# A two-layer streaming encoder: attention scores, transposes and values as a pipeline over query tiles

## The chip, the core and the metric

The kernel runs on one core of a Trainium2 chip. The metric is the device time of one execution in microseconds, the median over runs. The core's engines have queues of their own and meet through semaphores: TensorE (PE in the profile: matrix products, its weight loads shown apart as PEld), VectorE (DVE), ScalarE (ACT), GpSimd (POOL) and SyncE (SP), which here issues the DMAs. TensorE writes its results to PSUM, from where VectorE and ScalarE read them.

## What is computed

528 tokens (16 meta tokens and 512 others) of width 1024 pass through two layers in fp32. Each layer normalises, projects to many columns, and runs three branches of width 512, pooling, differential attention and RWKV-7 time mixing, which are gated, merged, projected and added; then comes a convolutional feed-forward block. The branch that matters here, cut to its core (4 heads, two maps c per head with 64 dimensions each, values of 128):

```python
q = partial_rope(q); k = partial_rope(k)          # (tokens, 4, 2, 64)
def block(qi, ci):                                # 128 queries at a time
    s = einsum('bqhcd,bkhcd->bhcqk', qi, k) * 64 ** -0.5
    s = where(chunk[keys] <= ci[queries], s, -inf)    # chunks of 64 tokens
    p = softmax(s)
    a = p[:, :, 0] - lam * p[:, :, 1]
    return einsum('bhqk,bkhe->bqhe', a, v)
o = rms_norm(o, subln_w, 1e-5) * (1.0 - lambda_init)
```

## The kernel before

Activations lie transposed, features on partitions and the 528 tokens along the free dimension. A projection (gemm, lines 137 to 153) multiplies weights split into a high and a low part of a reduced fp32 form (F32R) with activations split likewise: three products for each of 8 row blocks and each half of 264 tokens, 48 in all (24 for the branch projections, which have 4 row blocks). weights (lines 126 to 135) loads 512 columns by a DMA on SyncE's queue; ScalarE makes the high part, VectorE the low part. A gemm writes into one of two PSUM lanes, g and f, of one buffer each, or into the tile s.

attention_phase (line 225) runs through ATTORDER, a list of steps written out by hand. q is a head's three projections, with rope on q and k (head, rope); h its attention (attend); n normalises the heads that wait; w and m are a pooling window and its linear; r is renorm, which rebuilds the activations from the input, normalised; u0 and u1 are the branch projections (projections) of pooling and attention. The steps give priorities. A scheduler at build time fixes the order of each engine's queue: an instruction of a later step is put ahead of one of an earlier step that is not ready, as far as buffers allow. So the products of head h + 1 fill the gaps of the attention of head h.

attend transposes v and calls softmax_tile for the 16 meta queries (j = -1) and four tiles of 128 queries. For each tile and each of the two maps the scores are one fp32 product (two records in the profile) of 64 rows, the maps on partitions 0 to 63 and 64 to 127 (line 269); the last tile has 528 keys and needs two PSUM banks a map, so two rounds (line 285). VectorE masks with a memset, takes the maximum and scales it, ScalarE takes the exponential and the sum, VectorE inverts the sums, ScalarE scales the second map by the sum and -lambda (line 296), VectorE combines (line 297). Then TensorE transposes the result, the 16 meta keys apart (lines 300 and 307), ScalarE copies it to SBUF (302, 310), and TensorE multiplies by v: the meta keys as a product of 16 rows (311), the others as products of 128 (313). ScalarE squares for the norm, VectorE copies (316, 317). The scores' PSUM tile s has one buffer (pss), the tile c two (pc).

## Time and profile before

| | |
|---|---|
| median of 3 runs | 2026.38 us |
| lowest, highest | 2024.83, 2027.46 us |
| profiled execution | 2025.1 us, span 2023.3 us |
| TensorE busy | 1972.2 us, 97% of the span |
| VectorE busy | 1260.9 us, 62% |
| ScalarE busy | 903.6 us, 45% |
| GpSimd busy | 25.1 us, 1% |
| mean granted TensorE clock | 0.996 |

The profile is of one execution, so sums are made against its 2025.1 us. A group's busy time is the union of its instructions' times; a record of TensorE is longer than the distance to the next one's start, because products are pipelined. What a product costs is therefore read from the distance of starts in the timeline.

### The profile page before, as it was taken

The numbers are of one execution on the slowest core, as the hardware profiler recorded it, in microseconds if no ns is written. First come the engines' busy times: TensorE is split into PE (matmuls) and PEld (weight loads), VectorE is DVE, ScalarE is ACT, GpSimd is POOL, SyncE is SP. The second block draws the span as 40 slices with busy tenths as digits, with TensorE's granted clock in tenths as the row PEclk, the third lists the DMA queues.
The fourth block names the chain that finished last, engine by engine and source line by source line (L and its number), as shares of the span: only waits on it lengthen the run. The fifth ranks groups of instructions, "written<-read, shape, count | busy, mean of one in ns | idle before, by whom it ended". The sixth has DMA issues, their size and how long they took to land. (4 is left out here: it accounts for less than half of the span.)

```text
span 2023.3 us, 40763 instructions
## 1 busy us (share of the span) xinstructions
PE 1972.2 (97%) x16528; PEld 1843.4 (91%) x16528; DVE 1260.9 (62%) x2304; ACT 903.6 (45%) x1741; POOL 25.1 (1%) x138
## 2 busy tenths in 40 slices
PE   8999999999999999999999999999899999999998
PEld 7888987988899999999988889889889999999886
DVE  7676377864666777753366753779455667777532
ACT  5556355334434444432254564552343454444332
POOL 0000000000000000000000000010000000000000
PEclk9999999999999999999999999999899999999999
DMA  6114422452464222234342244234514652222332
GB/s 200 49 47 138 160 76 64 151 150 85 131 189 137 90 90 94 90 100 124 119 130 64 60 135 143 73 92 128 171 54 128 216 189 91 93 90 94 94 94 94
DMA packets 145068, 228.37 MB, mean 113 GB/s; under 512 B 35536, under 2 KB 45296, under 8 KB 144752
## 3 DMA queue, kind: packets, MB, share of 16 engines
q1 hardware_dynamic: 144880, 225.77, 35.6%
q8 instruction: 130, 2.13, 0.4%
q14 instruction: 58, 0.48, 0.1%
HBM read 190.94 MB, written 34.77 MB: 112 GB/s over the span
## 5 line engine op out<-in xcount | busy, mean ns | idle before, releaser
L133 ACT CAST whi<-raw 128x512 fp32r<-128x512 f32 x564 | 346.1, 616 | 687.8 <-PE f L150 260.3
L134 DVE TENSOR_TENSOR wlo<-raw,whi 128x512 fp32r<-128x512 f32 x564 | 384.6, 684 | 334.6 <-ACT whi L133 315.9
L150 PE MATMUL g<-xh,whi 128*128 128x264 f32 (+1 forms) x1632 | 343.1, 289 | 7.9 <-ACT whi L133 6.1
L150 PE MATMUL g<-xh,wlo 128*128 128x264 f32 (+1 forms) x1632 | 342.3, 288 | 0.0
L150 PE MATMUL g<-xl,whi 128*128 128x264 f32 (+1 forms) x1632 | 341.3, 288 | 0.7 <-DVE xl L179 0.7
L150 PE MATMUL f<-xh,wlo 128*128 128x264 f32 (+1 forms) x1472 | 311.0, 290 | 6.6 <-DVE wlo L134 6.6
L150 PE MATMUL f<-xl,whi 128*128 128x264 f32 (+1 forms) x1472 | 309.5, 288 | 1.2 <-issue 1.2
L150 PE MATMUL f<-xh,whi 128*128 128x264 f32 (+1 forms) x1472 | 306.8, 288 | 1.3 <-DVE pu L374 0.8
L150 PEld LDWEIGHTS g<-xh,whi 128*128 128x128 f32 x1632 | 256.1, 190 | 14.5 <-ACT whi L133 6.1
L150 PEld LDWEIGHTS g<-xh,wlo 128*128 128x128 f32 x1632 | 256.5, 190 | 5.9 <-issue 3.8
L150 PEld LDWEIGHTS g<-xl,whi 128*128 128x128 f32 x1632 | 255.5, 189 | 4.9 <-DVE xl L179 1.2
L150 PEld LDWEIGHTS f<-xh,wlo 128*128 128x128 f32 x1472 | 231.5, 190 | 14.8 <-DVE wlo L134 7.9
L150 PEld LDWEIGHTS f<-xl,whi 128*128 128x128 f32 x1472 | 231.3, 190 | 4.0 <-issue 1.5
L150 PEld LDWEIGHTS f<-xh,whi 128*128 128x128 f32 x1472 | 230.5, 190 | 3.8 <-DVE pu L374 1.0
L1001 DVE TENSOR_TENSOR u<-g,rstd 128x528 f32<-128x528 f32 (+1 forms) x44 | 30.9, 702 | 77.2 <-PE g L150 77.2
L1001 DVE TENSOR_TENSOR u<-f,rstd 128x528 f32<-128x528 f32 (+1 forms) x44 | 30.9, 702 | 31.2 <-PE f L150 31.2
L706 DVE TENSOR_TENSOR i<-i,i 128x1 f32<-128x1 f32 (+30 forms) x62 | 48.2, 778 | 1.5
L150 PE MATMUL g<-gb,whi 128*128 128x264 f32 (+1 forms) x256 | 42.4, 285 | 0.0
L150 PE MATMUL f<-gb,whi 128*128 128x264 f32 (+1 forms) x256 | 42.2, 285 | 0.0
L1016 ACT CAST ah<-cg 128x528 fp32r<-128x528 f32 (+1 forms) x44 | 27.7, 629 | 22.2 <-DVE cg L1014 22.2
L150 PE MATMUL g<-al,whi 128*128 128x264 f32 x176 | 35.9, 285 | 0.0
L150 PE MATMUL f<-al,whi 128*128 128x264 f32 x176 | 35.8, 285 | 0.0
(397 smaller groups left out, 3246.2 us busy)
## 6 DMA issues: line engine op xcount, KB each, us to landing
raw<-in_w_in_dram SPq DMA_DIRECT2D x216, 256.0 KB, 2.9
raw<-in_ffn_up_dram SPq DMA_DIRECT2D x176, 256.0 KB, 2.8
raw<-in_ffn_down_dram SPq DMA_DIRECT2D x84, 256.0 KB, 2.6
raw<-in_w_branch_dram SPq DMA_DIRECT2D x48, 256.0 KB, 2.7
raw<-in_w_out_dram SPq DMA_DIRECT2D x32, 256.0 KB, 2.9
md<-th SPq DMA_DIRECT2D x16, 264.0 KB, 2.1
mu<-md SPq DMA_DIRECT2D x8, 528.0 KB, 5.0
bon<-h SPq DMA_DIRECT2D x16, 264.0 KB, 2.0
```

Of the source, the lines that this page charges most:

```text
L133: nc.scalar.copy(hi, raw)
L134: nc.vector.tensor_tensor(lo, raw, hi.bitcast(F32), ALU.subtract)
L150: nc.tensor.matmul(ps[:, h, :nh], w[:, ks], x[k0 + k][:, c0 + h * nh:c0 + (h + 1) * nh], start=(k0 + k == 0 and j == 0), stop=(k0 + k == n ...
L706: nc.vector.tensor_tensor(tv, m[:lanes, 0:i, i].unsqueeze(1).broadcast_to([lanes, i, i]), xt[:lanes, 0:i, 0:i], ALU.mult)
L1001: nc.vector.tensor_tensor(B.v2(u[:, 2 + c0:]), ps, B.v2(rstd[:, c0:]), ALU.mult)
L1016: nc.scalar.copy(h, g)
```

## The change

softmax_tile goes. Its work is done by step, five of them per head, each with one chain of products that keep their order on TensorE (the manual dependencies named "one burst"): the scores of a tile, the values of the tile of three steps ago, in step 1 the transposes of v, and the transposes of the tile of two steps ago. step 0 does the first full tile and the meta queries together (with 128 query and 128 key columns for the latter, masked), steps 1 and 2 a tile each, steps 3 and 4 one map each of the last tile. normalise first runs steps without scores until the lag is empty.

Scores are now products over 128 rows in the reduced fp32 form. stacked puts the high part of a map's q on its own 64 partitions and the low part on the other 64. twice makes the high and the low part of k, and copies both to the other 64 partitions by a DMA on GpSimd's queue. Two products add up: with k's high part, and with its low part. The meta keys' values (vm) are padded with zeros to 128 rows. The maps are combined without the first scale (mix), which comes in when the values are read from PSUM, as a scale of the square and of the copy to o.

ATTORDER moves q3 and h3 ahead of normalise and of the pooling windows; there is one normalise for all four heads. The lanes of heads 1 to 3 alternate. Working tiles of rope, renorm and projections share one tag t with 6 buffers; the second weight pool has 2 raw buffers in place of 3.

The diff, without the removed body of softmax_tile and some removed lines of attend:

```diff
--- before.py
+++ after.py
@@ -245,109 +245,190 @@

         def rope(tidx, lane="g"):
             ps = B.gemm(B.ins["w_in"][l, tidx], xh, xl, 0, L, lane)
-            raw = T("qraw", 2)
+            raw = T("t", 6)
             nc.scalar.copy(B.v2(raw), ps)
-            q = T("q" if tidx < T_K else "k", 2)
+            q = T("t", 6)
             nc.vector.tensor_tensor(B.v2(q), ps, B.v2(ropec), ALU.mult)
-            sh = T("qsh", 2)
+            sh = T("t", 6)
             nc.vector.stream_shuffle(sh, raw, perm)
             nc.vector.tensor_tensor(sh, sh, ropes, ALU.mult)
             nc.vector.tensor_tensor(q, q, sh, ALU.add)
-            return q
...
+            return stacked(q) if tidx < T_K else twice(q)
+
+        LO, HI = slice(0, 64), slice(64, 128)
+
+        def stacked(q):
+
+            t = T("qs", 2, (128, 2, L), F32R)
+            for c, (own, other) in enumerate(((LO, HI), (HI, LO))):
+                nc.scalar.copy(t[own, c], q[own])
+                nc.vector.tensor_tensor(t[other, c], q[own], t[own, c].bitcast(F32), ALU.subtract)
+            return t
+
+        def twice(k):
+
+            t = T("ks", 2, (128, 2, 2, L), F32R)
+            for c, (own, other) in enumerate(((LO, HI), (HI, LO))):
+                nc.scalar.copy(t[own, c, 0], k[own])
+                nc.vector.tensor_tensor(t[own, c, 1], k[own], t[own, c, 0].bitcast(F32), ALU.subtract)
+                nc.gpsimd.dma_start(t[other, c], t[own, c])
+            return t
+
+        def scores(out, q, k, c, q0, keys):
+            return [nc.tensor.matmul(out, q[:, c, q0:q0 + 128], k[:, c, i, keys], start=(i == 0), stop=(i == 1))
+                    for i in range(2)]
+
+        qkv, waiting = {}, []
+        lag = [[], [], []]
+
+        def soft(S, c0, w, mask):
+
+            ps, e, sm, mx = S
+            for m in mask:
+                nc.vector.memset(m, NEG)
+            v = ps[:, :, c0:c0 + w]
+            nc.vector.tensor_reduce(mx, v, AX.X, ALU.max)
+            nc.vector.tensor_scalar(mx, mx, -0.125, None, ALU.mult)
+            for c in range(2):
+                nc.scalar.activation(e[c][:, :w], v[:, c], AF.Exp, bias=mx[:, c:c + 1], scale=0.125,
+                                     accum_out=sm[:, c:c + 1])
+
+        def mix(e, sm, w):
+
+            rs = T("rs", 8, (128, 2))
+            nc.vector.reciprocal(rs, sm)
+            nc.vector.scalar_tensor_tensor(rs[:, 1:2], rs[:, 1:2], nlam, sm[:, 0:1], ALU.mult, ALU.mult)
+            nc.vector.scalar_tensor_tensor(e[0][:, :w], e[1][:, :w], rs[:, 1:2], e[0][:, :w], ALU.mult, ALU.add)
+            return e[0], rs
+
+        def small():
+            return T("sm", 6, (128, 2)), T("mx", 4, (128, 2))
+
+        def step(H, i):
+
+
+            done = lag[2]
+            lag[2], lag[1], lag[0] = lag[1], lag[0], []
+            burst = []
+            ps = B.pss()
+            spare = [ps[:, b, 384:512] for b in range(2)]
+            new = []
+            if H:
+                q, k = H["qk"]
+                if i == 0:
+                    for c in range(2):
+                        burst += scores(ps[:, c, 0:144], q, k, c, META, slice(0, 144))
+                        burst += scores(ps[:, c, 144:272], q, k, c, 0, slice(0, 128))
+                elif i < 3:
+                    nk = META + 128 * (i + 1)
+                    for c in range(2):
+                        burst += scores(ps[:, c, :nk], q, k, c, META + 128 * i, slice(0, nk))
+                else:
                     for hf in range(2):
...
+                        burst += scores(ps[:, hf, :264], q, k, i - 3, META + 384, slice(hf * 264, hf * 264 + 264))
+            for t in done:
+                if "po" not in t["shared"]:
+                    t["shared"]["po"] = B.pc()
+                po = t["shared"]["po"][:, t["slot"]:t["slot"] + 128]
+                at, HH = t["at"], t["H"]
+                burst.append(nc.tensor.matmul(po, at[:, t["m"]:t["m"] + 128], HH["vm"], start=True, stop=not t["nb"]))
+                for b in range(t["nb"]):
+                    burst.append(nc.tensor.matmul(po, at[:, b * 128:b * 128 + 128], HH["vt"][:, b, :],
+                                                  start=False, stop=(b == t["nb"] - 1)))
+            if H and i == 1:
+                pv = B.pc()
+                v = H["v"]
+                for b in range(4):
+                    burst.append(nc.tensor.transpose(pv[:, b * 128:(b + 1) * 128],
+                                                     v[:, META + b * 128:META + (b + 1) * 128], B.ident))
+                burst.append(nc.tensor.transpose(spare[0], v[:, :128], B.ident))
+            if lag[2]:
+                pt = B.pc()
+                at = T("at", 2, (128, 640))
+                at_n = 0
+                for t in lag[2]:
+                    t["at"], t["m"] = at, t["off"] + t["nb"] * 128
+                    for b in range(t["nb"]):
+                        burst.append(nc.tensor.transpose(pt[:, b * 128:(b + 1) * 128],
+                                                         t["a"][:, META + b * 128:META + (b + 1) * 128], B.ident))
+                    dst = pt[:, t["m"]:t["m"] + 128] if t["m"] < 512 else spare[1]
+                    burst.append(nc.tensor.transpose(dst, t["a"][:, :128], B.ident))
+                    at_n = t["m"] + 128
+            for x, y in zip(burst, burst[1:]):
+                tc.add_manual_dep(y.ins, x.ins.name, mybir.DependencyInfo(
+                    mybir.DependencyClass.NoSync, mybir.DependencyReason.DATA), reason="one burst")
+
+            if H:
+                if i == 0:
+                    for c0, w, slot, mask in ((0, 144, 0, [ps[0:64, :, 80:144]]),
+                                              (144, 128, 128, [ps[:, :, 160:272]])):
+                        e = [T("e", 6), T("e", 6)]
+                        sm, mx = small()
+                        soft((ps, e, sm, mx), c0, w, mask)
+                        new.append((e, sm, w, slot))
+                elif i < 3:
+                    nk = META + 128 * (i + 1)
+                    e = [T("e", 6), T("e", 6)]
+                    sm, mx = small()
+                    soft((ps, e, sm, mx), 0, nk, [ps[0:64, :, nk - 64:nk]])
+                    new.append((e, sm, nk, 0))
+                else:
+                    c = i - 3
+                    if c == 0:
+                        H["wide"] = [T("e", 6), T("e", 6)], *small()
+                    e, sm, mx = H["wide"]
+                    nc.vector.memset(ps[0:64, 1, 200:264], NEG)
+                    nc.vector.tensor_reduce(mx[:, c:c + 1], ps[:, :, :264], AX.XY, ALU.max)
                     nc.vector.tensor_scalar(mx[:, c:c + 1], mx[:, c:c + 1], -0.125, None, ALU.mult)
...
+                    nc.scalar.activation(B.v2(e[c]), ps[:, :, :264], AF.Exp, bias=mx[:, c:c + 1],
                                          scale=0.125, accum_out=sm[:, c:c + 1])
...
+                    if c:
+                        new.append((e, sm, L, 0))
+            if H and i == 1:
+                H["vt"] = T("vt", 2, (128, 4, 128))
+                H["vm"] = T("vm", 2, (128, 128))
+                nc.gpsimd.memset(H["vm"], 0.0)
+                nc.scalar.copy(H["vt"], pv.rearrange("p (a b) -> p a b", a=4))
+                nc.scalar.copy(H["vm"][:META], spare[0][:META])
+            if lag[2]:
+                nc.scalar.copy(at[:, :min(at_n, 512)], pt[:, :min(at_n, 512)])
+                if at_n > 512:
+                    nc.scalar.copy(at[:, 512:], spare[1])
+            for t in done:
+                po = t["shared"]["po"][:, t["slot"]:t["slot"] + 128]
+                junk = T("junk", 1, (128, 128))
+                j, HH = t["j"], t["H"]
+                nc.scalar.activation(junk, po, AF.Square, scale=t["rs"][:, 0:1], accum_out=HH["ss"][:, j:j + 1])
+                nc.vector.tensor_scalar(HH["o"][:, j, :], po, t["rs"][:, 0:1], None, ALU.mult)
+            shared = {}
+            for e, sm, w, slot in new:
+                a, rs = mix(e, sm, w)
+                meta = slot == 128
+                lag[0].append(dict(a=a, rs=rs, H=H, shared=shared, slot=slot, nb=0 if meta else (w - META) // 128,
+                                   off=256 if meta else 0, j=0 if meta else (w - META) // 128))

         def head(h):
-            q = rope(T_Q + h)
-            k = rope(T_K + h, "g" if h else "f")
-            ps = B.gemm(B.ins["w_in"][l, T_V + h], xh, xl, 0, L, "g" if h else "s")
+            q = rope(T_Q + h, None if h else "g")
+            k = rope(T_K + h, None if h else "f")
+            ps = B.gemm(B.ins["w_in"][l, T_V + h], xh, xl, 0, L, None if h else "s")
             v = T("v", VB)
             nc.vector.tensor_tensor(B.v2(v), ps, B.v2(rstd), ALU.mult)
             qkv[h] = q, k, v

         def attend(h):
             q, k, v = qkv.pop(h)
...
             if not waiting:
                 waiting.append(T("ss", 2, (128, 4, 5)))
                 nc.gpsimd.memset(waiting[0], 1.0)
...
+            H = dict(qk=(q, k), v=v, o=T("o", OB, (128, 5, 128)), ss=waiting[0][:, len(waiting) - 1])
+            waiting.append((h, H["o"]))
+            for i in range(5):
+                step(H, i)

         def normalise():

+            while any(lag):
+                step(None, 0)
             rs = waiting.pop(0)
             nh = len(waiting)
             nc.scalar.activation(rs[:, :nh], rs[:, :nh], AF.Sqrt, bias=B.eps[1e-5], scale=1.0 / 128)
@@ -357,9 +438,10 @@
                 ss = rs[:, hi]
                 for j in range(5):
                     nq = 128 if j else META
-                    nc.vector.tensor_scalar(o[:nq, j, :], o[:nq, j, :], ss[:nq, j:j + 1], None, ALU.mult)
+                    nc.vector.tensor_scalar(o[:, j, :], o[:, j, :], ss[:, j:j + 1], None, ALU.mult)
                     c = (0, META, META + 128, 0, 128)[j]
-                    nc.tensor.transpose(pt[:, j // 3, c:c + nq], o[:nq, j, :], B.ident[:nq, :nq])
+
+                    nc.tensor.transpose(pt[:, j // 3, c:c + 128], o[:, j, :], B.ident)
                 w0 = META + 256
                 for i, (c, w) in enumerate(((0, w0), (w0, 256))):
                     B.split(bh[1][h][:, c:c + w], bl[1][h][:, c:c + w], pt[:, i, :w], sub)
@@ -395,7 +477,7 @@
         def renorm():

             for d in range(KT):
-                x = T("xr", 2)
+                x = T("t", 6)
                 nc.sync.dma_start(x, xsrc(d))
                 nc.vector.scalar_tensor_tensor(x, x, vec[:, V_NM + d:V_NM + d + 1], rstd, ALU.mult, ALU.mult)
                 h, lo = B.xtile("xh"), B.xtile("xl")
@@ -409,7 +491,7 @@
             for d in range(KT):
                 lane, pool = ("f", ap) if d % 2 else ("g", None)
                 up = B.gemm(B.ins["w_branch"][l, br, d], bh[br], bl[br], c0, n, lane, pool)
-                t = T("th", 3)[:, :n]
+                t = T("t", 6)[:, :n]
                 nc.scalar.copy(B.v2(t), up)
                 nc.sync.dma_start(merged_dram[d][:, br, :n], t)

@@ -969,12 +1051,12 @@
 ORDER = 'k0 k1 k2 k3 l0 n0 d0 i0 o0 p0 i1 d1 o1 p1 i2 d2 o2 p2 i3 d3 o3 p3 l1 g0 g1 g2 g3'
 MAINBUFS = (4, 3, 3)
 FILLBUFS = (3, 2, 2)
-WIDEBUFS = (3, 3, 3)
+WIDEBUFS = (2, 3, 3)
 CUT = 304
 WL = 3
 VB = 2
 OB = 4
-ATTORDER = 'q0 s0 h0 q1 h1 q2 h2 n0 w0 w1 m0 w2 m1 w3 m2 m3 q3 h3 n0 u0 r0 u1'
+ATTORDER = 'q0 s0 h0 q1 h1 q2 h2 q3 h3 n0 w0 w1 m0 w2 m1 w3 m2 m3 u0 r0 u1'

```

## Rows read from the trace of the kernel before

**Rows 1.** The page, part 1: busy time and share, instructions.
```profile
PE 1972.2 (97%) x16528; PEld 1843.4 (91%) x16528; DVE 1260.9 (62%) x2304; ACT 903.6 (45%) x1741; POOL 25.1 (1%) x138
```

**Rows 2.** Sums by stretch: stretch, its length, busy time per engine, clock, DMA.
```profile
24.40:220.90 196.50, 192.29 (x1400) 169.69 (x1399) 128.51 (x325) 105.35 (x280) 1.15 (x12) 1.00 0.29 94
1022.70:1223.40 200.70, 197.29 (x1451) 175.29 (x1450) 129.90 (x327) 107.26 (x282) 1.39 (x15) 1.00 0.31 98
300.00:350.00 50.00, 45.23 (x389) 39.25 (x387) 39.22 (x68) 27.72 (x51) 2.72 (x7) 1.00 0.23 66
350.00:400.00 50.00, 50.00 (x400) 48.97 (x400) 40.15 (x101) 17.87 (x32) 3.05 (x6) 1.00 0.47 149
1366.00:1416.00 50.00, 50.00 (x418) 50.00 (x417) 48.11 (x101) 14.57 (x25) 0.00 (x0) 1.00 0.41 127
```

**Rows 3.** Groups by form, TensorE, 24.4 to 220.9 us: count, busy, mean ns, idle.
```profile
L313 PE MATMUL c<-vt,at 128*128 128x128 f32 x80 | 11.9, 279 | 0.0
L285 PE MATMUL s<-k,q 64*128 64x264 f32 x32 | 9.2, 409 | 0.0
L311 PE MATMUL c<-vm,atm 16*128 16x128 f32 x32 | 7.7, 321 | 0.0
...
L269 PE MATMUL s<-k,q 64*128 64x400 f32 x16 | 3.8, 548 | 0.0
L269 PE MATMUL s<-k,q 64*128 64x272 f32 x16 | 2.9, 441 | 0.0
L269 PE MATMUL s<-k,q 64*128 64x144 f32 x16 | 2.1, 335 | 0.1
L311 PE MATMUL c<-vm,atm 16*16 16x128 f32 x8 | 1.5, 273 | 0.0
L269 PE MATMUL s<-k,q 64*16 64x16 f32 x16 | 0.9, 180 | 0.9 <-ACT vm L339 0.9
```

**Rows 4.** Timeline of TensorE: start, length of the group, line, form, records.
```profile
31.42 0.41 PE L150 MATMUL g<-xh,whi 128*128 128x264 f32 x2
...
35.57 0.22 PE L269 MATMUL s<-k,q 64*16 64x16 f32 x4 [0.93 <-ACT vm L339]
...
77.97 0.28 PE L150 MATMUL f<-xh,wlo 128*128 128x264 f32 x1
78.18 0.94 PE L269 MATMUL s<-k,q 64*128 64x400 f32 x4
79.05 0.39 PE L150 MATMUL f<-xh,wlo 128*128 128x264 f32 x1
79.28 0.28 PE L150 MATMUL f<-xh,whi 128*128 128x264 f32 x1
...
80.45 0.48 PE L311 MATMUL c<-vm,atm 16*128 16x128 f32 x2
80.86 0.39 PE L150 MATMUL g<-xh,whi 128*128 128x264 f32 x1
...
84.44 1.15 PE L285 MATMUL s<-k,q 64*128 64x264 f32 x4
```

**Rows 5.** Timeline of TensorE: the end of layer 0's stretch, and the last stage.
```profile
220.47 0.40 PE L150 MATMUL f<-bh,wlo 128*128 128x264 f32 x2
220.72 0.41 PE L150 MATMUL g<-xh,whi 128*128 128x264 f32 x2
...
1900.10 0.39 PE L1056 MATMUL g<-whi,ah 128*128 128x512 f32 x1
1900.33 0.40 PE L1056 MATMUL g<-whi,al 128*128 128x512 f32 x1
```

**Rows 6.** Groups by form, VectorE, 24.4 to 220.9 us.
```profile
L134 DVE TENSOR_TENSOR wlo<-raw,whi 128x512 fp32r<-128x512 f32 x45 | 30.9, 687 | 22.3 <-ACT whi L133 20.3 <-PE f L150 1.8
L403 DVE TENSOR_TENSOR xl<-xr,xh 128x528 fp32r<-128x528 f32 x8 | 5.6, 697 | 0.0
```

**Rows 7.** The page, part 6: DMA issues, count, KB each, us to landing.
```profile
md<-th SPq DMA_DIRECT2D x16, 264.0 KB, 2.1
```

More of the change, by code (lines that the diff above doesn't have):

```diff
@@ L311, in softmax_tile @@
-            nc.tensor.matmul(po[:nq, :128], atm[:, :nq], vm, start=True, stop=(nb == 0))
-            for b in range(nb):
-                nc.tensor.matmul(po[:, :128], at[:, b * 128:(b + 1) * 128], vt[:, b, :],
-                                 start=False, stop=(b == nb - 1))
-            junk = T("junk", 1, (128, 128))
-            nc.scalar.activation(junk[:nq], po[:nq, :128], AF.Square, accum_out=ss[:nq, j + 1:j + 2])
-            nc.vector.tensor_copy(o[:nq, j + 1, :], po[:nq, :128])
-        qkv, waiting = {}, []
+                    if c:
+                        new.append((e, sm, L, 0))
@@ L330, in attend @@
             q, k, v = qkv.pop(h)
-            pv = B.pss()
-            nc.tensor.transpose(pv[:META, 1, :128], v[:, :META], B.ident)
-            for b in range(4):
-                nc.tensor.transpose(pv[:, 0, b * 128:(b + 1) * 128],
-                                    v[:, META + b * 128:META + (b + 1) * 128], B.ident)
-            vt = T("vt", 2, (128, 4, 128))
-            vm = T("vm", 2, (META, 128))
-            nc.scalar.copy(vt, pv[:, 0, :].rearrange("p (a b) -> p a b", a=4))
-            nc.scalar.copy(vm, pv[:META, 1, :128])
-            o = T("o", OB, (128, 5, 128))
             if not waiting:
@@ L343, in attend @@
                 nc.gpsimd.memset(waiting[0], 1.0)
-            ss = waiting[0][:, len(waiting) - 1]
-            waiting.append((h, o))
-            for j in (-1, 0, 1, 2, 3):
-                softmax_tile(h, q, k, vt, vm, o, ss, j)
+            H = dict(qk=(q, k), v=v, o=T("o", OB, (128, 5, 128)), ss=waiting[0][:, len(waiting) - 1])
+            waiting.append((h, H["o"]))
+            for i in range(5):
+                step(H, i)
         def normalise():
+            while any(lag):
+                step(None, 0)
             rs = waiting.pop(0)
```

50 lines of the change are left out of this document (removed).

## The prediction

> **What bounds the kernel now.** I read the page's busy shares first: TensorE is busy for 97% of the span, no other engine for more than 62% [rows 1]. Then the sums by stretch, for the two attention stretches that the change touches: from the end of the norm's products to the last branch projection, 196.5 us in layer 0 and 200.7 us in layer 1, 397 us of 2023 [rows 2]. [...] TensorE is idle for only 196.50 - 192.29 = 4.2 us and 200.70 - 197.29 = 3.4 us of them, VectorE is busy for 65%. So the order of work by now hides the softmax behind products of the next head, and what is left to win is TensorE work itself, plus at most 7.6 us of idle time.
>
> A product of the projections costs 0.25 us for two of 264 columns, 0.122 us each [rows 5]. Sixteen gemms of 48 and sixteen of 24 make 1152 such products, 140 us of a stretch; the other 57 us are attention. The groups by form show what they are [rows 3]: the scores take 0.9 + 2.1 + 2.9 + 3.8 + 9.2 = 18.9 us a layer, the products of the 16 meta keys 7.7 + 1.5 = 9.2 us, the other values 11.9 us. The timeline adds what the groups don't show [rows 4]: the 64-row block of 77.97 to 79.28 starts 0.21 us after a single projection product (normal 0.12) and the single one after it keeps the next one waiting 0.23 us. So each 64-row block costs about 0.09 us going in and 0.10 us coming out, less some 0.07 us by which its last record outlasts the start of the next product.
>
> **The change part by part.** *Scores.* Per head the kernel before has six blocks. With 0.12 us of edges each, a layer's 24 cost 18.9 + 2.9 = 21.8 us. After, a tile's scores are two full-array products in the reduced fp32 form for each of two maps: high and low part of q stacked in 128 rows, against k's high and then its low part. No row shows such a product of scores, but the projections are of the same form: 0.122 us at 264 columns, and 0.23 us at 512 in the last stage [rows 5], so 0.00045 us a column between; this gives 0.125 us at 272 and 0.18 at 400. Below 264 columns nothing of this form is shown: between half of it, 0.06 us (columns alone), and 0.122 us (no gain from fewer columns); I take 0.10. A head then has 8 x 0.10 (first block and meta together) + 4 x 0.125 + 4 x 0.18 + 8 x 0.122 = 3.0 us, between 2.7 and 3.2. A layer: 12 us. Gain 9.8 us.
>
> *Meta keys.* The 16-row products come in 20 blocks a layer; the one at 80.45 lasts 0.41 us, with edges of about 0.2 us [rows 4]. 9.2 + 20 x 0.2 = 13.2 us. After, the meta rows are padded with zeros to 128 (vm), and each tile has one more ordinary fp32 product of two records. Eighty records of the other values took 11.9 us; with pipelining, their starts stand some 0.11 us apart, so 40 more cost 4.5 us. Gain 8.7 us.
>
> *Transposes, normalise.* Their number stays the same; the 16-row ones become full ones and no longer break the stream, and values and transposes now follow each other in one run. I put that at 1.5 us a layer (0 to 3). Together 20 us a layer, **40 us** in all, between 36 and 44.
>
> *What is added beside TensorE.* stacked and twice run four times each per layer, with two ScalarE copies and two VectorE subtractions of 528 columns each: 16 subtractions at 0.70 us, the row of the same form in renorm [rows 6], 11 us a layer. The meta tile is computed on 128 rows instead of 16 and has a larger mask: some 1.5 us more. ScalarE gets 16 copies and loses the 20 scalings of e and the 20 copies of atm; it comes out even. VectorE's load is what matters, so I work it out for the part of the stretch ahead of renorm and the projections. It has 128.5 us in all [rows 2]; renorm makes two rounds of eight operations, the one shown 5.6 us, so 11 us; the projections' weights are 16 of 45, 11 us [rows 6]. 106 are left, and 118.5 with what is added. TensorE needs there 196.5 - 16 x 24 x 0.122 = 149.7 us now, of it 4.2 idle; after 149.7 - 4.2 - 20 = 125.5. **VectorE goes from 71% to 94% of that part, if TensorE is never to wait.** This is where I expect part of the gain to go. How TensorE fares beside such a VectorE is seen in three stretches [rows 2]: VectorE at 78% and TensorE at 90% (300 to 350 us), 80% and 100% (350 to 400), 96% and 100% (1366 to 1416, where VectorE works on something TensorE needs only later). The new part resembles the first most, since each step goes from TensorE to VectorE to ScalarE and back, but it has more spare products to fill with. I take 93%: 125.5 / 0.93 = 135, 9.5 us of idle time a layer, 19 us in place of the 7.6 us now.
>
> *What is moved.* q3, k3 and v3 go ahead of the pool windows. Their weight loads go ahead of the windows' in SyncE's queue too, with the same number of loads; a transfer of this size takes about 2.1 us [rows 7], a gemm of two loads 5.8 us, so nothing waits for them. WIDEBUFS gives the windows one raw buffer less; two still hold a whole window's weights. What the move takes away is cover: every window and its pool linear use lane f, and behind the last window no head's products are left; window, sums and linear are a chain of some 4 to 5 us, which the last head's late steps and its transposes cover if they are still there. It is part of the 9.5 us. Head 0 starts later, by four copies and subtractions, about 4.5 us, and k's copy to the other half of the partitions. That is two transfers a head of 264 KB on GpSimd's queue. No row shows a transfer from there; on SyncE's queue that size takes the same 2.1 us, and I take twice that as the upper end. First scores at 35.6 us now [rows 4] would come at about 43; the products of head 1 last from 31.4 us to 49, so it stays covered, and from head 1 on the copies lie a whole head ahead. Behind them on GpSimd wait only small memsets (GpSimd is busy for 1.2 us of the stretch [rows 2]).
>
> **The sum** is made against the profiled execution, 2025.1 us (span 2023.3); the median of the runs is 1.3 us above it. 2025.1 - 40 - 7.6 + 19 = 1996.5. I say **1996 us**.
>
> **The rivals.** *A, the forecast*: TensorE stays the bound at a share of 88 to 99% of the part: 2025.1 - 40 - 7.6 + 2 x (1.3 to 17), 1980 to 2012; with the bounds of 36 and 44 us it reaches 1976. *B, VectorE takes over*: at a share of 85% for TensorE the idle time is 22 us a layer, 2021 us; centre 2013. The 94% speak for it; against it that VectorE's 96% was reached once beside a full TensorE [rows 2].
>
> *C, slower: the single scores buffer.* pss has one buffer, so scores of step i + 1 wait until both exponentials of step i have read theirs. From the scores at 78.18 to the next at 84.44 are 6.3 us [rows 4], the longest steps of a head. Head 0 starts at 43 us, and 20 steps, 2 to 3 to drain the lag, normalise (some 8 us) and the second half of the projections (23.4 us) follow: 43 + 23 P + 31.4. It equals the present end, 220.7 us, at P = 6.4 us a step. At 6.8 us the stretch is 10 us longer in each layer, 2045. For it: VectorE's queue is fuller, and the longest period now is near that. Against it: a step's own chain (scores 0.7, mask, maximum, two exponentials of 0.6 us and more) is 3 to 4 us, and the transposes and values no longer stand in it.
>
> *D, the products don't get cheaper*: the pairs of 64-row products now run partly side by side (four records of 400 columns in 0.87 us [rows 4]), and the change gives that up; if the new products cost like fp32 ones, twice as much, a head's scores would take 5.5 to 6 us, the 9.8 us a layer are gone, and 1996 becomes 2016. The rows of the projections speak against it. [...]
>
> [...]
>
> **How the numbers follow.** A 0.60, B 0.20, C 0.11, D 0.05, E 0.04. Below 1976 lies some 0.03 of A, above 2019 a fifth of B and all of C: the range 1976 to 2019 leaves out 0.18. A measurement of this kernel can tell 0.2%, 4 us, from no change. Of C some 0.03 and of B 0.02 fall within it: faster 0.87, same 0.05, slower 0.08.
>
> **What would show it.** Right: groups of scores in 128*128 form, eight products of 264 columns a head some 0.12 us apart; no 0.09 us ahead of them; stretches of 175 to 190 us; TensorE work lower by some 20 us each. For B, VectorE above 90% until renorm, and TensorE's waits put down to it. For C, starts of scores over 6 us apart, with ScalarE's exponentials as releaser. For D, starts 0.22 us apart. [...] Wrong altogether: time lost outside the two stretches, by a lower granted clock.

## The result and the profile after

| | before | after |
|---|---|---|
| median, in the same session | 2026.92 us | 2036.79 us (2033.87 to 2043.70) |
| profiled execution, its span | 2025.1, 2023.3 us | 2042.5, 2040.7 us |
| mean granted TensorE clock | 0.996 | 0.983 |

The ratio is 1.0058, with an interval of 1.0035 to 1.0081: slower by 0.6%. The forecast was 1996 us. The six executions spread by 10 us and go roughly with their granted clock, from 2033.9 us at 0.987 to 2043.7 at 0.982; the profiled one, 0.983, is the second longest, so it lost more to the clock than the median did.

The page, part 1, of the kernel after (busy time, share of the span, instructions):

```profile
PE 1962.8 (96%) x16528; PEld 1863.7 (91%) x16528; DVE 1286.2 (63%) x2342; ACT 898.9 (44%) x1695; POOL 34.2 (2%) x160
```

TensorE is busy for 9 us less than in [rows 1], yet the span is 17 us longer. So TensorE waits more, and the mean clock says that part of its busy time runs slower. The sums by stretch show where (stretch, length, busy time of PE, PEld, DVE, ACT and POOL with their counts, granted clock, DMA share, GB/s). The kernel after: both attention stretches, then layer 0's in three parts, then two short pieces of it.

```profile
24.40:229.80 205.40, 185.78 (x1400) 177.97 (x1399) 140.92 (x344) 103.75 (x257) 4.87 (x13) 0.95 0.33 100
1032.30:1239.80 207.50, 190.84 (x1446) 183.10 (x1445) 143.02 (x346) 104.43 (x259) 5.22 (x17) 0.95 0.35 105
24.40:138.00 113.60, 106.49 (x838) 103.25 (x837) 93.93 (x240) 68.07 (x190) 4.73 (x11) 0.98 0.30 88
138.00:183.00 45.00, 35.63 (x218) 31.28 (x217) 27.76 (x70) 16.19 (x35) 0.14 (x2) 0.85 0.15 45
183.00:229.80 46.80, 43.66 (x349) 43.44 (x348) 19.24 (x34) 19.49 (x34) 0.00 (x0) 0.96 0.54 181
145.50:148.90 3.40, 3.40 (x18) 3.40 (x18) 0.00 (x0) 0.75 (x2) 0.14 (x2) 0.50 0.00 0
172.80:183.10 10.30, 8.05 (x30) 6.52 (x30) 3.40 (x7) 1.82 (x3) 0.00 (x0) 0.50 0.16 48
```

The same three parts of the kernel before:

```profile
24.40:138.00 113.60, 110.78 (x787) 94.83 (x785) 78.29 (x204) 60.54 (x177) 0.22 (x2) 1.00 0.24 75
138.00:183.00 45.00, 43.79 (x321) 38.83 (x320) 38.03 (x89) 27.79 (x68) 0.10 (x1) 1.00 0.42 129
183.00:220.90 37.90, 37.72 (x297) 36.03 (x296) 12.19 (x34) 17.02 (x35) 0.83 (x9) 1.00 0.32 111
```

The stretches last 205.4 and 207.5 us, against 196.5 and 200.7 in [rows 2]; the rest of the kernel is the same within 2 us. The middle part, where now all pool windows stand, has 45.0 - 35.6 = 9.4 us of idle TensorE against 1.2, and a clock of 0.85 against 1.00. In the last two pieces the clock is 0.50: there a pair of projection products takes 0.44 us from start to start (179.29 to 179.73, below), at the full clock 0.24 (183.17 to 183.41). In the kernel before the clock is 1.00 throughout these stretches [rows 2].

For each stretch I count idle time, half of the busy time at the lower level (the loss), and the rest, which is work at the full clock. This is worked out from all records of TensorE in the stretches above, layer 0 / layer 1, in us. (Half is a little much: 0.44 against 0.24 us makes it 0.45, that is, 16 us of loss in all instead of 8.96 + 8.86 = 17.8.)

| kernel | length | idle | lost to the clock | work |
|---|---|---|---|---|
| before | 196.5 / 200.7 | 4.2 / 3.4 | 0 / 0 | 192.3 / 197.3 |
| after | 205.4 / 207.5 | 19.6 / 16.7 | 9.0 / 8.9 | 176.8 / 182.0 |

So the work fell by 15.4 us a layer, as the change is meant to do; 15.4 and 13.3 us of idle time and 9 us of lower clock came in. What TensorE waits for in the middle part (engine, line, releaser: us in total, times, longest), in the view of waits:

```profile
PE f L163 <- DVE pu L456: 2.4, 2, 1.8
PE f L150 <- DVE bl L179: 2.0, 2, 1.8
PE g L150 <- ACT bh L178: 1.6, 2, 0.8
PE s L444 <- DVE bl L179: 1.6, 2, 1.1
PE f L163 <- DVE pp L468: 1.5, 1, 1.5
```

L150 is gemm, L163 pool_linear, L456 and L468 are pool_window, L444 normalise. pu is a window's product as VectorE read it from PSUM, pp its finished sums; bh and bl are the high and low part that ScalarE and VectorE make of a linear or of normalise's transposes. So a window waits for lane f, which the last linear holds until VectorE has read it, and the linear waits for the window's sums. VectorE's load is no bound there: it is busy for 27.8 of 45 us. The last two linears in the timeline of TensorE (start, length of the group, in brackets the idle time ahead of it), at the end of which lie the two starts 0.44 us apart:

```profile
169.76 1.16 PE L163 MATMUL f<-pp,pool_w 128*128 128x264 f32 x4 [1.81 <-DVE pu L456]
171.71 0.51 PE L150 MATMUL g<-bh,whi 128*128 128x264 f32 x2 [0.79 <-ACT bh L178]
172.52 0.58 PE L150 MATMUL g<-bl,whi 128*128 128x264 f32 x2 [0.29 <-DVE bl L179]
...
174.99 2.10 PE L163 MATMUL f<-pp,pool_w 128*128 128x264 f32 x4 [1.46 <-DVE pp L468]
177.88 0.81 PE L150 MATMUL g<-bh,whi 128*128 128x264 f32 x2 [0.79 <-ACT bh L178]
...
179.29 0.64 PE L150 MATMUL g<-bh,wlo 128*128 128x264 f32 x2
179.73 0.64 PE L150 MATMUL f<-bh,whi 128*128 128x264 f32 x2
```

The groups by form, TensorE, 24.4 to 229.8 us, which answer [rows 3]:

```profile
L278 PE MATMUL s<-ks,qs 128*128 128x264 f32 x32 | 6.0, 308 | 0.4 <-ACT e L383 0.2
L278 PE MATMUL s<-ks,qs 128*128 128x400 f32 x16 | 3.9, 365 | 0.2 <-ACT at L396 0.2
L278 PE MATMUL s<-ks,qs 128*128 128x272 f32 x16 | 3.1, 315 | 2.8 <-DVE e L301 2.0 <-ACT e L293 0.8
```

And a burst in the timeline of TensorE (start, length of the group), which answers [rows 4]:

```profile
66.84 0.40 PE L150 MATMUL f<-xh,wlo 128*128 128x264 f32 x2
67.08 0.75 PE L278 MATMUL s<-ks,qs 128*128 128x264 f32 x4
67.66 0.38 PE L334 MATMUL c<-vm,at 128*128 128x128 f32 x2
...
68.66 0.27 PE L355 MATMUL c<-consts,e 128*128 128x128 f32 x1
68.69 0.49 PE L150 MATMUL f<-xh,whi 128*128 128x264 f32 x2
69.02 0.40 PE L150 MATMUL f<-xl,whi 128*128 128x264 f32 x2
```

The four scores take 0.58 us to the next start; the first pair of projection products behind the burst takes 0.33 instead of 0.24, but starts only 0.03 us behind the last transpose.

### The profile page after: what moved, and what is told of

It reads as the page before. It is cut to its first block, busy times and chain, and to the rows that moved or that the text cites. A ratio compares the mean times of both kernels' runs of the same rounds, so it can differ in the third digit from the quotient of the medians.

```text
span 2040.7 us, 40772 instructions
## 1 busy us (share of the span) xinstructions
PE 1962.8 (96%) x16528; PEld 1863.7 (91%) x16528; DVE 1286.2 (63%) x2342; ACT 898.9 (44%) x1695; POOL 34.2 (2%) x160
## 4 chain that ended last, share of the span: by engine, by line
PE 81%; DVE 11%; ACT 3%; issue 3%; DMA 2%; SPq 0%; POOL 0%; DVEq 0%; ACTq 0%; POOLq 0%
PE f L150 33%; PE g L150 30%; PE g L1138 3%; PE f L1138 3%; DVE wlo L134 2%; DVE i L788 1%; PE s L163 1%; PE s L278 1%; PE c L997 1%; DVE q L690 1%; DVE i L790 1%; PE s L977 1%; DMA ks<-ks 1%; ACT whi L133 1%; PE c L981 1%
## 5 line engine op out<-in xcount | busy, mean ns | idle before, releaser
L134 DVE TENSOR_TENSOR wlo<-raw,whi 128x512 fp32r<-128x512 f32 x564 | 384.1, 683 | 364.9 <-ACT whi L133 343.8
L150 PE MATMUL f<-xh,wlo 128*128 128x264 f32 (+1 forms) x1616 | 339.4, 290 | 7.9 <-DVE wlo L134 7.9
L150 PE MATMUL f<-xh,whi 128*128 128x264 f32 (+1 forms) x1616 | 340.6, 291 | 5.2 <-DVE bl L179 2.9
L150 PE MATMUL f<-xl,whi 128*128 128x264 f32 (+1 forms) x1616 | 340.5, 290 | 0.0
L150 PE MATMUL g<-xh,whi 128*128 128x264 f32 (+1 forms) x1488 | 308.6, 287 | 6.7 <-ACT whi L133 6.7
L150 PE MATMUL g<-xh,wlo 128*128 128x264 f32 (+1 forms) x1488 | 310.6, 288 | 0.0
L150 PE MATMUL g<-xl,whi 128*128 128x264 f32 (+1 forms) x1488 | 308.1, 287 | 0.6 <-DVE xl L179 0.6
L150 PEld LDWEIGHTS f<-xh,wlo 128*128 128x128 f32 x1616 | 256.3, 192 | 12.3 <-DVE wlo L134 9.2
L150 PEld LDWEIGHTS f<-xh,whi 128*128 128x128 f32 x1616 | 256.5, 192 | 8.4 <-DVE bl L179 3.5
L150 PEld LDWEIGHTS f<-xl,whi 128*128 128x128 f32 x1616 | 256.5, 192 | 2.3 <-issue 0.4
L150 PEld LDWEIGHTS g<-xh,whi 128*128 128x128 f32 x1488 | 233.0, 190 | 8.7 <-ACT whi L133 6.7
L150 PEld LDWEIGHTS g<-xh,wlo 128*128 128x128 f32 x1488 | 233.5, 190 | 2.9 <-issue 0.9
L150 PEld LDWEIGHTS g<-xl,whi 128*128 128x128 f32 x1488 | 232.5, 189 | 3.0 <-DVE xl L179 1.0
L1083 DVE TENSOR_TENSOR u<-g,rstd 128x528 f32<-128x528 f32 (+1 forms) x44 | 30.9, 702 | 53.4 <-PE g L150 53.4
L278 PE MATMUL s<-ks,qs 128*128 128x144 f32 (+3 forms) x192 | 35.3, 310 | 9.1 <-DMA ks<-ks 3.7
L150 PE MATMUL g<-gb,whi 128*128 128x264 f32 (+1 forms) x256 | 42.7, 286 | 0.0
L150 PE MATMUL f<-gb,whi 128*128 128x264 f32 (+1 forms) x256 | 42.2, 285 | 0.0
L278 PEld LDWEIGHTS s<-ks,qs 128*128 128x128 f32 x192 | 26.9, 192 | 14.5 <-ACT e L293 6.7
L150 PE MATMUL g<-bh,whi 128*128 128x264 f32 (+1 forms) x128 | 28.9, 310 | 10.8 <-ACT t L495 6.2
```

What stands on the lines that cost most here:

```text
L134: nc.vector.tensor_tensor(lo, raw, hi.bitcast(F32), ALU.subtract)
L150: nc.tensor.matmul(ps[:, h, :nh], w[:, ks], x[k0 + k][:, c0 + h * nh:c0 + (h + 1) * nh], start=(k0 + k == 0 and j == 0), stop=(k0 + k == n ...
L278: return [nc.tensor.matmul(out, q[:, c, q0:q0 + 128], k[:, c, i, keys], start=(i == 0), stop=(i == 1)) for i in range(2)]
L1083: nc.vector.tensor_tensor(B.v2(u[:, 2 + c0:]), ps, B.v2(rstd[:, c0:]), ALU.mult)
```

## The experiments

All ratios are to the kernel before, run in the same session; a1, b1 and so on are the runs. The theory after the result: the pipeline saves what it should, and the move of head 3 ahead of the windows, with the lanes that go with it, leaves TensorE without other products in the windows' part; the gaps then bring the lower clock. Rivals: VectorE's added work; the shared buffers t; GpSimd's copy of k.

**Order.** The changed kernel with the windows ahead of head 3, one normalise:

```diff
-ATTORDER = 'q0 s0 h0 q1 h1 q2 h2 q3 h3 n0 w0 w1 m0 w2 m1 w3 m2 m3 u0 r0 u1'
+ATTORDER = 'q0 s0 h0 q1 h1 q2 h2 w0 w1 m0 w2 m1 w3 m2 m3 q3 h3 n0 u0 r0 u1'
```

> The changed kernel with the pooling windows back ahead of head 3 (one normalise, after head 3). Theory 'cover': the changed kernel loses its time where the windows, all in lane f, run behind the last head with nothing beside them; in layer 0 TensorE idles 9 to 10 us between 125 and 180 us and the granted clock is at the lower level for 13.7 us there. Then this kernel is faster than the changed one by 2 x (9 idle + about 5 clock), some 28 us: 2005 to 2015 us against 2037, and faster than the kernel before by 10 us or more. Theory 'VectorE': the loss is VectorE's load of the pipeline, wherever the windows stand: 2030 us or more, with the idle time only moved.

Run a1: 2036.84 us, 1.0046 (1.0031 to 1.0061): as slow as the changed kernel. In its waits of layer 0 a linear now waits once for 4.5 us, ahead of k's copy:

```profile
PE f L163 <- DVE pp L468: 4.5, 1, 4.5
PE s L278 <- DMA ks<-ks: 4.1, 3, 2.3
```

Idle time is 21.1 and 15.4 us, as much as with the new order. So the order alone isn't what costs.

The kernel before with the changed kernel's order, and nothing else of the change:

```diff
-ATTORDER = 'q0 s0 h0 q1 h1 q2 h2 n0 w0 w1 m0 w2 m1 w3 m2 m3 q3 h3 n0 u0 r0 u1'
+ATTORDER = 'q0 s0 h0 q1 h1 q2 h2 q3 h3 n0 w0 w1 m0 w2 m1 w3 m2 m3 u0 r0 u1'
```

> The kernel before with the new order alone (windows behind head 3, one normalise), the old softmax tiles kept. Theory 'cover': the windows stand uncovered here too, slower than before by 8 to 25 us, with TensorE idle ahead of the pool linears and a lower clock there. Theory 'VectorE': VectorE has its old load, so within 5 us of before.

Run b1: 2062.53 us, 1.0173 (1.0156 to 1.0190). In the old pipeline the move alone costs 35 us: idle 14.8 and 13.0 us, 6.2 and 5.0 us lost to the clock, work nearly as before (192.5 and 198.4). The part of the windows:

```profile
24.90:138.00 113.10, 111.34 (x801) 95.94 (x800) 76.19 (x195) 59.15 (x176) 0.11 (x1) 1.00 0.24 76
138.00:190.00 52.00, 39.78 (x232) 31.17 (x232) 37.84 (x103) 25.34 (x68) 0.70 (x7) 0.89 0.16 47
```

Ahead of it all is as it was; in the 52 us TensorE idles for 12.2, and the clock is down. So the move makes such gaps without the pipeline too.

**Order and lanes.** Windows ahead of head 3, and q, k and v of heads 1 to 3 in lane g as before:

```diff
-            q = rope(T_Q + h, None if h else "g")
-            k = rope(T_K + h, None if h else "f")
-            ps = B.gemm(B.ins["w_in"][l, T_V + h], xh, xl, 0, L, None if h else "s")
+            q = rope(T_Q + h)
+            k = rope(T_K + h, "g" if h else "f")
+            ps = B.gemm(B.ins["w_in"][l, T_V + h], xh, xl, 0, L, "g" if h else "s")
```

> The changed kernel with the pooling windows back ahead of head 3 and with the projections of heads 1 to 3 in lane g again, as before; one normalise. With the order alone put back, the windows in lane f stood in the way of head 3's projections, which took that lane in turn. Theory 'cover', now as 'two lanes beside each other': windows in f beside head 3 in g keep TensorE fed; idle time of a stretch falls from 16 to 21 us to 8 to 12, the lower clock goes, 2005 to 2020 us. Theory 'VectorE': idle stays at 15 us or more, 2030 us or more.

Run a9: 2017.61 us, 0.9964 (0.9951 to 0.9976): 19 us less than the changed kernel. Layer 0's stretch and its middle part:

```profile
24.40:215.40 191.00, 178.91 (x1399) 172.91 (x1398) 141.40 (x344) 103.60 (x257) 4.97 (x13) 0.99 0.35 108
...
138.00:183.00 45.00, 43.48 (x345) 41.72 (x345) 28.68 (x83) 26.06 (x69) 1.13 (x3) 1.00 0.33 102
```

The middle part has 1.5 us of idle time in place of 9.4, and a full clock. Why the old order needs the old lanes is seen at the last two linears of layer 0, which stand at nearly the same time in both runs. In a1:

```profile
129.85 0.40 PE L150 MATMUL g<-xh,wlo 128*128 128x264 f32 x2
130.81 1.16 PE L163 MATMUL f<-pp,pool_w 128*128 128x264 f32 x4 [0.56 <-DVE pu L456]
136.43 2.10 PE L163 MATMUL f<-pp,pool_w 128*128 128x264 f32 x4 [4.46 <-DVE pp L468]
140.12 0.81 PE L150 MATMUL f<-xh,whi 128*128 128x264 f32 x2 [1.59 <-DVE bl L179]
```

In a9:

```profile
130.91 1.16 PE L163 MATMUL f<-pp,pool_w 128*128 128x264 f32 x4
131.70 0.60 PE L150 MATMUL g<-xl,whi 128*128 128x264 f32 x2
...
136.28 0.28 PE L150 MATMUL g<-xl,whi 128*128 128x264 f32 x1
136.62 1.13 PE L163 MATMUL f<-pp,pool_w 128*128 128x264 f32 x4
```

In both VectorE makes the last window's sums from 130.1 us to 136.3 (a1) and 136.5 (a9). In a9 the products of head 3 in lane g fill this time. In a1 lane g's products of head 3 are done at 130 us, its other two gemms have lane f, and the first of them starts only when the last linear has been read from f: 4.5 and 1.6 us idle. With the order of before as a whole (two normalises) it is the same (run a10):

```diff
+ATTORDER = 'q0 s0 h0 q1 h1 q2 h2 n0 w0 w1 m0 w2 m1 w3 m2 m3 q3 h3 n0 u0 r0 u1'
```

> The same with normalise called twice, exactly the order of the kernel before; the pipeline runs empty once more in the middle. Theory 'two lanes': like the run with one normalise, 2005 to 2020 us, and a little better if the late normalise is what head 3 waits for. Theory 'VectorE': 2030 us or more.

Run a10: 2018.57 us, 0.9962 (0.9950 to 0.9975). The fourth corner, the three lines of lanes above put back alone and the order left new:

> The changed kernel with only the lanes of heads 1 to 3 put back (q, k and v of these heads in lane g), its order left as it is, the windows behind head 3. It fills the fourth corner beside after (new order, new lanes, 2037), the kernel with the old order and new lanes (2037) and the one with both old (2018). Theory 'the two belong together': the old lanes need windows in lane f between the heads' gemms; with all windows at the end, the gemms of heads 1 to 3 follow each other in one lane and each waits until ScalarE and VectorE have read the one ahead of it: about 9 gemms a layer, 1 to 2 us each, so 2037 + 2 x (9 to 18) = 2055 to 2073, as the old kernel with the new order lost 35 us. Rival 'the alternating lanes are what costs': undoing them alone brings most of the 19 us, 2018 to 2025.

Run c1: 2045.46 us, 1.0098 (1.0069 to 1.0127). The four corners:

| | new lanes | old lanes |
|---|---|---|
| new order | 1.0058 | 1.0098 |
| old order | 1.0046 | 0.9964 |

Either edit alone brings nothing, both together bring 1%; with the old lanes the move costs the pipeline 28 us (c1 against a9). The verdict of c1 is the first theory's, but neither its size (2055 to 2073) nor its mechanism: the waits of 138 to 183 us are those of normalise and of the last window, not of gemms that follow each other in one lane. The last product of a head or a window is made at 160.5 us there; behind it only linears, normalise and projections are left.

```profile
PE s L444 <- DVE bl L179: 4.5, 2, 2.2
PE g L150 <- ACT bh L178: 2.4, 3, 0.8
PE s L444 <- DVE pp L467: 1.1, 1, 1.1
```

**Lanes of the windows.** Windows and linears of the changed kernel alternate between f and g:

```diff
-            ps = B.gemm(..., *(("g", None) if g > WL else ("f", ap)))
+            ps = B.gemm(..., *(("g", None) if g % 2 else ("f", ap)))
-            ps = B.fmm(B.psg("f"), poolw[:, g * 128:(g + 1) * 128], pooled, L)
+            ps = B.fmm(B.psg("gf"[(g + 1) % 2]), poolw[:, g * 128:(g + 1) * 128], pooled, L)
```

> The changed kernel, in its own order, with the windows taking lanes f and g in turn and each pool linear the lane of the other. Theory 'two lanes': most of the 9 us of idle time in the windows' tail goes and the lower clock after it, 2 x (6 to 12), 2012 to 2026 us. Theory 'VectorE': no gain over 5 us, since the sums of a window run on VectorE either way.

Run a4: 2035.85 us, 1.0051 (1.0038 to 1.0064): no gain. Idle is 17.6 and 20.5 us; in layer 0 normalise's transposes (4.5 us, for VectorE's bl) and the wait of a projection for its lane's copy behind renorm (3.3) lead. So the single lane of the windows is not the cause by itself.

**VectorE's load.** In the attention stretches the low part of the weights is not made:

```diff
         nc.scalar.copy(hi, raw)
+        if self.nolo:
+            return hi, hi
         nc.vector.tensor_tensor(lo, raw, hi.bitcast(F32), ALU.subtract)
```

> The changed kernel, in its own order, without VectorE's low part of the weights in the attention stretches: the products with it take the high part again, so TensorE has the same work, and VectorE loses 45 subtractions, 31 us of 141 us in each stretch. (The result then lacks the low part of these weights.) Theory 'VectorE': with its load at 110 us TensorE's idle time falls from 18 us to 8 us or less and the lower clock with it: 2005 to 2015 us. Theory 'cover': the windows' tail and the start of head 0 stay, idle 13 us or more, 2025 us or more.

Run a11: 2032.52 us, 1.0030 (1.0021 to 1.0040). VectorE falls from 141 and 143 to 118 us a stretch, below the 128.5 of before, and the idle time only from 19.6 and 16.7 to 14.3 and 12.3 us: 9.7 of the 28.7 us that the change added. VectorE's load is the smaller part of it.

**VectorE's work on GpSimd.** The 16 subtractions of stacked and twice:

```diff
-                nc.vector.tensor_tensor(t[other, c], q[own], t[own, c].bitcast(F32), ALU.subtract)
+                nc.gpsimd.tensor_tensor(t[other, c], q[own], t[own, c].bitcast(F32), ALU.subtract)
```

> The changed kernel with the 16 subtractions of stacked and twice per layer made by GpSimd instead of VectorE, which takes 11 us of 141 us off VectorE in each attention stretch. Theory 'VectorE': idle time falls by most of that, 2015 to 2025 us. Theory 'cover': the windows' tail stays as it is, within 6 us of the changed kernel, or slower if GpSimd's subtraction is so long that k comes late.

Run a6: 2054.53 us, 1.0134 (1.0117 to 1.0150): 18 us slower. A group of GpSimd, layer 0, in this run:

```profile
L273 POOL TENSOR_TENSOR ks<-t,ks 64x528 fp32r<-64x528 f32 x8 | 11.3, 1416 | 24.9 <-ACT ks L272 24.6
```

In the changed kernel VectorE made one of them in 0.70 us:

```profile
L273 DVE TENSOR_TENSOR ks<-t,ks 64x528 fp32r<-64x528 f32 x8 | 5.6, 700 | 0.2
```

On GpSimd one takes 1.42 us. It stands ahead of k's copy, and the scores of layer 0 wait for that copy for 5.4 us. And VectorE's busy time fell only from 140.9 to 138.8 us, though 11 us went away.

**The buffers.** The projections' copies get buffers of their own in the changed kernel:

```diff
-            raw = T("t", 6)
+            raw = T("t", 4)
...
-                t = T("t", 6)[:, :n]
+                t = T("th", 2)[:, :n]
```

> The changed kernel with the shared working tiles parted: four for rope and renorm, two of their own for the branch projections. In the changed kernel one projection product waits 3.1 us per layer for the copy of a lane, which stands behind renorm's use of the shared tiles, and a stretch of lower clock follows. If the sharing causes this wait, it goes: 2 x (3 + 1.5), 5 to 10 us faster than the changed kernel. If the wait has another cause (order of the queues alone), within 3 us of it.

Run a3: 2044.72 us, 1.0081 (1.0063 to 1.0098). The wait of 3.1 us behind renorm is gone, and idle time is 22.4 and 19.9 us: waits of 3.8 us in normalise and 3.7 and 3.3 us at the linears take its place. So the shared buffers are not the cause either.

**What comes on top of order and lanes.** The same split of buffers in the version with old order and lanes, once with one normalise and once with two, and then k's copy issued by SyncE:

```diff
-                nc.gpsimd.dma_start(t[other, c], t[own, c])
+                nc.sync.dma_start(t[other, c].bitcast(F32), t[own, c].bitcast(F32))
```

> The pipeline with the old order (one normalise) and old lanes, 2018, in which the buffers that rope, renorm and the projections share are split (four for rope and renorm, two for the projections' copies). In it TensorE waits 3.5 us for a projection's copy behind renorm in layer 0. If the sharing is the cause and nothing takes its place: 2018 less 3 us a layer and less 1 to 2 us of lower clock behind it, 2010 to 2014. If the copy waits because ScalarE and VectorE are full with renorm then, the wait stays or moves: 2016 to 2020, as it was in the changed kernel itself.

Run c2: 2020.69 us, 0.9968 (0.9956 to 0.9981), no gain.

> The same split of buffers with the order of the kernel before (two normalises), 2019 without the split. Same expectations: 2011 to 2015 if the sharing is the cause, 2016 to 2020 if the wait moves.

Run c3: 2013.44 us, 0.9932 (0.9910 to 0.9955), 5 us less than a10; the intervals of the two overlap.

> As the one with one normalise and split buffers, and the copy of k to the other half of the partitions issued by SyncE in place of GpSimd. If the 3.3 us that the copy takes to land from GpSimd's queue, or its wait to be issued, sets head 0's start: first scores 1 to 2 us earlier in each layer, 2 to 4 us less than the version without it. Rival: on SyncE's queue the copy stands in order among the loads of weights and waits for VectorE's halves of k there, so loads behind it come late: 0 to 10 us more.

Run c4: 2010.97 us, 0.9923 (0.9899 to 0.9947), the lowest median here. Its two stretches, of its fastest execution:

```profile
24.60:213.90 189.30, 179.19 (x1399) 171.80 (x1398) 140.17 (x344) 102.39 (x257) 1.56 (x14) 1.00 0.34 109
1016.70:1208.00 191.30, 183.95 (x1450) 177.45 (x1449) 141.40 (x346) 104.17 (x259) 1.58 (x14) 1.00 0.36 114
```

The first scores come at 43.99 us, against 45.66 without SyncE's copy: the size expected. The gain of 10 us is more than that. In the profiled executions, 12 us apart, some 3.5 us lie outside the stretches and 4 us in them are lower clock, which this execution of c4 has none of. The copy itself lands no sooner (DMA issues: count, KB each, us to landing):

```profile
ks<-ks SPq DMA_DIRECT2D x16, 264.0 KB, 3.6
```

> The pipeline with order, lanes and two normalises of the kernel before, split buffers, and k's copy issued by SyncE. Without the last it took 2013; with one normalise the copy on SyncE's queue brought 10 us (2021 to 2011). If that comes from head 0's start and is independent of the order: 2003 to 2009. If it came from the chance of where the gaps of one normalise fall: 2011 to 2015.

Run c5: 2012.43 us, 0.9921 (0.9909 to 0.9934): 1 us below the version without it, so the 10 us of c4 were not the copy's own price. Much of them may be the clock: c4's six executions go from 2007.4 us at 0.997 to 2016.5 at 0.990, and those of c2 have 0.988 to 0.993. Why the clock falls less there stays open.

> The changed kernel, its order and lanes kept, with split buffers and k's copy issued by SyncE: the two extras that the version with the old order and lanes (2011) has beside the pipeline. If the loss stems from order and lanes, the extras bring no more than there (2 to 10 us): 2030 to 2040. Rival, the extras were what made that version fast, whatever the order: 2012 to 2025.

Run d1: 2037.78 us, 1.0047 (1.0031 to 1.0062). With the new order and lanes both extras bring nothing: they are no part of the cause.

**The clock.** Useless products ahead of each window and linear of the changed kernel:

```diff
+        def fill(n):
+            pf = B.pc()
+            f = [nc.tensor.matmul(pf, xh[i % 4][:, :128], xh[4 + i % 4][:, :512], start=True, stop=True)
+                 for i in range(n)]
...
+            fill(7)
             ps = B.fmm(B.psg("f"), poolw[:, g * 128:(g + 1) * 128], pooled, L)
```

> The changed kernel with useless products added on TensorE ahead of each pool window and each pool linear: seven of 512 columns each time, 54 a layer, about 0.23 us each, 12.4 us a layer, into a PSUM buffer that nobody reads. They lie where TensorE has its idle gaps of 138 to 180 us (9.3 us in layer 0) and where 13.6 us at the lower clock are recorded. Theory 'the clock falls because TensorE stood idle': with the gaps filled the granted clock stays at 1.00 in that part, the 6 us a layer lost there come back, and although 12.4 us of work are added, the time is 2037 + 2 x (12.4 - 9 - 6), 2030 to 2037. Rival 'the clock falls for another cause (where the kernel stands, what it does there)': the lower clock stays, and the time is 2037 + 2 x (12.4 - 9), 2043, up to 2060 if the products fill none of the gaps.

Run d2: 2043.52 us, 1.0082 (1.0068 to 1.0096). (The products are 56 a layer, eight times seven.) The time is the rival's; the rows of layer 0 are the theory's. With the products, the whole stretch, then 165 to 183 us:

```profile
24.10:226.00 201.90, 190.81 (x1455) 182.27 (x1455) 140.98 (x344) 103.98 (x257) 4.87 (x13) 0.99 0.33 102
...
165.00:183.00 18.00, 16.79 (x116) 15.22 (x115) 8.39 (x17) 4.57 (x8) 0.00 (x0) 1.00 0.19 58
```

The changed kernel itself, the same 18 us:

```profile
165.00:183.00 18.00, 12.86 (x60) 10.42 (x59) 8.02 (x14) 3.75 (x6) 0.00 (x0) 0.72 0.26 79
```

Idle 1.2 us in place of 5.1, clock 1.00 in place of 0.72. Layer 0's stretch got 3.5 us shorter with 12.3 us more work: 8.5 us of idle time and 7.3 us of lower clock went. In layer 1 the products fell into fewer gaps, 4.7 us of idle time and 1.3 us of lower clock went for 11.7 us of work, and the stretch is 5.6 us longer. So where the gaps were filled, the clock stayed up; that the gaps cause all 9 us a layer is not shown. Two of the four pieces of layer 0 at 0.50 lie outside the windows' part in the changed kernel: 53.4 to 56.8 us, behind a wait of head 0's scores of 2.0 us, and 210.4 to 213.8 us, from the end of the wait of 3.1 us behind renorm on.

## Why the prediction was wrong

The sum was 2025.1 - 40 - 7.6 + 19. Measured, in the same terms: - 30.8 of work, - 7.6 + 36.3 of idle time, + 17.8 of lower clock, + 1.7 outside the stretches: 2042.5, which is the profiled execution.

**The sum has no term for the clock**, and that missed 17.8 us, the most of any term in this execution. At the 1.00 of [rows 2] there was nothing to gain. I did not ask whether there was something to lose: that full clock went with a TensorE that idled for 2% of the time, and I had forecast more gaps myself. As a sign of being wrong I named a lower clock outside the stretches; there the time at 0.50 is 28 us against 18 before, in them 41 against none. The longest such piece of layer 0, from 172.8 to 183.1 us, comes behind waits of 1.8, 0.8 and 0.3 us for VectorE and ScalarE.

**"What the move takes away is cover … It is part of the 9.5 us"** failed by most of the other 17.3 us. The chain of window, sums and linear was seen, but "the last head's late steps and its transposes cover" it was an assumption. The windows' part has 9.4 us idle in layer 0, as much as I gave the whole stretch. The chain is also longer than the 4 to 5 us that I gave it: in a9, at full clock, the last window's products end at 130 us, its sums at 136.5, and lane f is free after its linear at 139.3, 9 us. I should have put a price on each of four windows. b1 shows that price without the pipeline (35 us), a9 that it goes with order and lanes together. Why it needs both: a step has spare products to fill with when another head's gemms are still to do and have a lane that the windows don't hold; the new order takes away the first, the new lanes the second. a1 shows the second at the last two linears (4.5 and 1.6 us idle, which a9 fills), c1 the first, where nothing of a head or a window is left from 160.5 us on. This is shown for these waits of layer 0, not for every wait of the 36.3 us.

The 9.5 us of idle time themselves, and the 93% behind them, were near for a kernel that keeps its order and lanes. a9, which differs from the changed kernel in nothing else, has 12.1 and 10.8 us, and still loses 1.7 and 3.4 us to the clock: 2025.1 - 30.2 - 7.6 + 22.9 + 5.1 + 2.3 = 2017.6. c4, with two edits more and in its fastest execution, has 10.1 and 7.4 us and no lower clock in the stretches.

**"Together 20 us a layer"** was 15.4 (15.1 in a9, 13.1 and 13.3 in c4, so the term is known to some 2 us). The widths were sized well: eight products of 128 and 144 columns take 0.84 us (70.97 to 71.81), 0.105 each where I took 0.10. I took the edges of the old blocks off and gave the new bursts none. By the starts of the bursts at full clock, going in costs some 0.10 us, a delay and a longer first product together, and coming out some 0.01: 0.11 us, about 2.4 us a layer with 22 bursts. Transposes and normalise gave 0.4 instead of 1.5 us, and the values cost 0.6 more. The remaining 0.5 us I can't place.

**The rivals.** B did not come: ahead of 183 us VectorE is busy for 121.7 us (118.5 was the estimate) of 158.6, 77%, and taking 23 us a layer off it (a11) gained 4 to 6 us in all. C did not: the starts of the scores are 4.9 us apart on average in layer 0 and 5.2 in layer 1; over 6.4 are three in layer 0 (8.5 and 7.4 at head 0, and 6.9) and four in layer 1 (9.5 at head 0, and 7.1 to 7.5). D did not: four products in 0.58 us with the edge. E, the chance of 0.04 for a late copy of k, was small: the copy is waited for 0.9 us at head 0 in layer 0 and 2.2 us in layer 1. Issued by GpSimd it lands in 3.3 us, by SyncE (c4) in 3.6:

```profile
ks<-ks POOLq DMA_DIRECT2D x16, 264.0 KB, 3.3
```

The chance of 0.08 for slower was too low, since I let only C stand for that side. The loss of cover, which the text names, had a place and no point from which it decides: a window's chain minus the products that are left to run beside it.

## What to carry to other kernels

Where an engine is busy for 97%, the order of its work is part of the speed: a change that makes the work cheaper and moves it at the same time should be tried as two changes, the moves last. Price each move by what is left to run beside the chain that loses its cover, chain by chain. And where TensorE has run at full clock while it hardly waited, new idle time may bring the lower clock with it: here 29 us more of it came with 18 us of loss. That is no fixed rate: a1 has as much idle time and lost 10 us.

## What was not expected of the hardware

- TensorE spends 69 us of the span at a granted clock of 0.50, 41 of them in the attention stretches, with TensorE busy for 90% and 92% of these. The kernel before has 18, none of them there.
- In a6 VectorE is slower beside GpSimd: its subtraction of a weight's low part (L134) takes 0.78 us on average in layer 0's stretch, against 0.69 in the changed kernel. Over the whole run it took 1.14 us in the 16 cases that overlap one of GpSimd's, and 0.68 in the 548 others. Nine of the 16 start while GpSimd subtracts, and end 0.55 to 0.61 us after GpSimd; the seven that start first take 0.67 to 0.69.
- A subtraction of 64 rows and 528 columns costs GpSimd 1.42 us and VectorE 0.70, and VectorE takes as much for 128 rows ([rows 6]).
